# Projections chunk by chunk, a gating stage in another order, and an attention with ScalarE and VectorE in program order

## The chip, the cores and the metric

The kernel runs on one core of a Trainium2 chip. The metric is the device time in microseconds, as the median of several runs. TensorE (PE in the profile) does the matmuls and reads its weights with separate loads (PEld), VectorE (DVE) and ScalarE (ACT) do the elementwise work and read the matmuls' results, GpSimd (POOL) takes a part of the elementwise work in on-chip memory, and SyncE (SP) issues all transfers to and from HBM.

## What is computed

A trunk of two layers over 1024 latent tokens and 256 context tokens, 1024 wide, in float32. Both layers have the form x = layer_norm(alpha x + gate y).

```python
# layer 0: recurrent unit and spatial gating unit
p = h @ w_in                                   # 5 parts of 512
y_a = h_rec * silu(p[..., W:2 * W])            # bidirectional linear scan h_rec
u, v = gelu(p[..., 2 * W:3 * W]), gelu(p[..., 3 * W:4 * W])
y_b = spatial_gating(u, v) * silu(p[..., 4 * W:5 * W])
y = concatenate([y_a, y_b]) @ w_out
# layer 1: gated convolution and differential attention, 4 heads
p = h @ w_in                                   # 8 parts of 512
s = einsum('bqhmd,bkhmd->bhmqk', q, k) * d ** -0.5     # m = 0, 1
a = softmax(s[:, :, 0]) - lam * softmax(s[:, :, 1])
o = einsum('bhqk,bkhe->bqhe', a, v)            # k, v: context and latent tokens
y = concatenate([conv branch, rms_norm(o) * silu(gate)]) @ w_out
```

## The kernel before, in words

Every float32 operand of a matmul is split into two parts, a rounded one (hi, made by ScalarE) and the rest (lo, made by VectorE or GpSimd as a difference: `split`, L134). A product is then three matmuls: hi by hi, hi by lo, lo by hi. The input of a layer lies on chip with its features on the partitions: 8 blocks of 128 features (k), 1280 tokens in three chunks of 256, 512 and 512 (`CHUNKS`, L28).

A projection of 128 output features takes 8 x 3 x 3 = 72 matmuls. `proj3_g` (L158) runs over k outside, over the three products, and over the three chunks inside; it is used in layer 0. `proj1_g` (L170) does one chunk and runs over k; the keys and everything in layer 1 use it. `wload` (L143) loads the weights of a projection (512 KB, two raw buffers) and splits them in two halves of four k-blocks each, with four buffers of hi and four of lo; ScalarE makes hi, GpSimd lo.

TensorE issues in the order of the program text (`manual_schedule` at L55). The order on the other engines comes from a scheduler that simulates the program; nested regions at L305 and L514 fix SP's order as well. In such a region an engine issues its instructions in the order of the text.

Layer 0. `lru_x`, `lru_g` and `lru_rec` do the recurrent unit for four groups of features; `interleave` (L483) puts the steps of the modulation (`mod_step`) into the projections' gaps. Then the gating: z of group 0 (L520), the value weights (`vweights`), ten tiles of 128 tokens of v (`sgu_v`, L540, TensorE 24 matmuls a tile), the spatial products (`sgu_s`, L555) between them, the u projection of group 1 (L583) with the last spatial products inside, and then z of group 1, u and z of groups 2 and 3 (L620 to L627). Their results lie in two PSUM buffers of three banks (`pj3`).

Layer 1. Keys and values are projected and written to HBM. The attention (L1013) runs over 34 steps; step i of the first 32 is one block of 128 queries of a head, 8 blocks a head, in pairs that share their loaded queries (`load_q`, L902: two maps, hi and lo). `scores(i, m)` (L935) is six matmuls into one PSUM tile of three banks (psc, a single buffer), the row maximum on VectorE (L944) and the exponential on ScalarE (L946), which frees the tile. After m = 1 the two exponentials are combined on VectorE (L948 to L950, L1043). `trans(i - 1, .., j)` (L954) transposes the combined block before in three parts (4, 4 and 2 transposes; atr) and splits them (ah by ScalarE, al by VectorE). `av` (L968) multiplies a finished pair by the values; `finish1` to `finish3` normalise and gate half a head. `fill(us)` (L916) puts steps of the other projections (`proj_qg`, `conv_branch`) between, by the amounts in `FL` (L912); a step is three matmuls and counts 0.65 us. So a block has 0.1, 1.2, 1.0 and 0.5 us of fill around its three transpose steps, and either 1.3 with `av` or 4.7 between its two scores: 5.8 in the mean. Each weight is loaded where its projection begins. `load_k` and `load_v` load into one buffer (kd) and split at once.

## Time and profile before

| | us |
|---|---|
| median of 3 runs | 1170.89 (1170.02 to 1172.15) |
| span of the profiled execution | 1170.5 |
| layer 0, recurrent unit, until the z projection of group 0 | 0 to 209 |
| gating | 209 to 383 |
| output projection of layer 0, keys and values of layer 1 | 383 to 613 |
| attention with the other projections | 613 to 1071 |
| output projection of layer 1 | 1071 to 1170 |

The profile follows one execution. Its span of 1170.5 us is 0.4 under the median of the runs. Matmuls are pipelined: the profile gives each one from its start to its modelled end, so neighbours overlap, and the distance from start to start is the pace. PEclk is the clock that TensorE was granted, as a share of 2.4 GHz (0.5 is 1.2 GHz). A wait is given in brackets behind the instruction that waited, with what released it.

### The profile page before, as it was taken

What the parts mean: (1) busy time and instruction counts of PE and PEld (TensorE: products, weight loads), DVE (VectorE), ACT (ScalarE), POOL (GpSimd) and SP (SyncE); (2) the same over time, 40 slices, a digit from 0 to 9 for tenths busy, and PEclk for the clock granted to TensorE, in tenths of its full rate; (3) what the DMA queues carried; (4) which work ended last, traced back from release to release, by engine and by line L of the source; (5) the groups of instructions that cost most, each with busy time, mean ns of one, the idle gap of its engine ahead of it and who ended that gap; (6) DMA issues with size and microseconds to landing.
All of it is one profiled execution on the core that took longest, in us unless ns stands there. A gap on an engine that the chain in (4) does not pass through costs nothing.

```text
span 1170.5 us, 14967 instructions
## 1 busy us (share of the span) xinstructions
PE 1132.6 (97%) x5842; PEld 922.0 (79%) x5842; DVE 738.9 (63%) x1007; ACT 440.2 (38%) x685; POOL 329.6 (28%) x200
## 2 busy tenths in 40 slices
PE   6999999899999999999999899999999999999997
PEld 3667777678888888888887788788888788888776
DVE  5677986943411475636104668876777877738897
ACT  3453654621121234342113455544544554413110
POOL 1114212620240132258104311221121321221971
PEclk9999999999999999999999999999999999999999
DMA  9654551230332444243215411322221510126622
GB/s 373 239 182 142 180 176 41 73 130 1 120 104 71 144 139 147 96 136 140 77 45 162 113 55 54 95 76 84 77 76 37 146 62 19 46 72 249 218 99 82
DMA packets 71606, 133.93 MB, mean 114 GB/s; under 512 B 6368, under 2 KB 34912, under 8 KB 70640
## 3 DMA queue, kind: packets, MB, share of 16 engines
q1 hardware_dynamic: 71536, 132.97, 34.3%
q8 instruction: 46, 0.75, 0.3%
q14 instruction: 24, 0.20, 0.1%
HBM read 105.67 MB, written 27.28 MB: 114 GB/s over the span
## 4 chain that ended last, share of the span: by engine, by line
PE 83%; DVE 8%; DMA 3%; ACT 3%; issue 2%; POOL 0%; SPq 0%; POOLq 0%; DVEq 0%; ACTq 0%
PE px L164 5%; PE pu L164 5%; PE pg L164 5%; PE p L174 5%; PE p L175 5%; PE p L176 5%; PE pout L648 4%; PE pout L646 4%; PE pout L647 4%; PE pz L164 4%; PE psc L942 3%; PE pv L198 3%; PE pv L199 3%; PE pv L200 3%; PE psc L943 3%; PE atr L965 3%
## 5 line engine op out<-in xcount | busy, mean ns | idle before, releaser
L141 POOL TENSOR_TENSOR wlo<-wraw,whi 128x512 fp32r<-128x512 f32 x92 | 148.1, 1615 | 458.5 <-ACT whi L138 449.8
L648 PE MATMUL pout<-woh,ylo 128*128 128x512 f32 (+1 forms) x296 | 114.5, 387 | 3.1 <-DVE ylo L141 3.1
L946 ACT ACTIVATE e<-psc,st 128x1280 f32<-128x1280 f32 x64 | 85.1, 1329 | 85.6 <-DVE st L944 85.6
L646 PE MATMUL pout<-woh,yhi 128*128 128x512 f32 (+1 forms) x296 | 114.8, 388 | 0.2
L647 PE MATMUL pout<-wol,yhi 128*128 128x512 f32 (+1 forms) x296 | 114.0, 385 | 0.0
L944 DVE TENSOR_REDUCE st<-psc 128x1 f32<-128x1280 f32 x64 | 95.0, 1485 | 27.8 <-PE psc L943 27.7
L138 ACT ACTIVATE whi<-wraw 128x512 fp32r<-128x512 f32 x92 | 57.2, 628 | 134.3 <-PE p L175 27.7
L174 PE MATMUL p<-hhl,whi 128*128 128x512 f32 x256 | 106.8, 417 | 0.0
L176 PE MATMUL p<-hhl,wlo 128*128 128x512 f32 x256 | 100.7, 393 | 0.0
L175 PE MATMUL p<-hll,whi 128*128 128x512 f32 x256 | 100.5, 393 | 0.0
L942 PE MATMUL psc<-k,qh 128*128 128x512 f32 (+1 forms) x192 | 68.0, 369 | 8.4 <-ACT e L946 8.4
L943 PE MATMUL psc<-k,ql 128*128 128x512 f32 (+1 forms) x192 | 69.3, 361 | 0.0
L138 ACT ACTIVATE ah<-atr 128x512 fp32r<-128x512 f32 (+1 forms) x96 | 48.5, 525 | 51.6 <-PE atr L965 50.6
L648 PEld LDWEIGHTS pout<-woh,ylo 128*128 128x128 f32 x296 | 55.6, 188 | 15.3 <-DVE ylo L141 4.0
L646 PEld LDWEIGHTS pout<-woh,yhi 128*128 128x128 f32 x296 | 55.6, 188 | 12.1 <-DVE zt L610 0.5
L647 PEld LDWEIGHTS pout<-wol,yhi 128*128 128x128 f32 x296 | 55.7, 188 | 11.5
L138 ACT ACTIVATE yhi<-yraw 128x512 fp32r<-128x512 f32 x36 | 22.5, 630 | 103.7 <-PE pout L647 57.6
L141 DVE TENSOR_TENSOR al<-atr,ah 128x512 fp32r<-128x512 f32 (+1 forms) x96 | 55.6, 594 | 5.8 <-ACT ah L138 5.6
L176 PEld LDWEIGHTS p<-hhl,wlo 128*128 128x128 f32 x256 | 48.2, 188 | 10.7
L175 PEld LDWEIGHTS p<-hll,whi 128*128 128x128 f32 x256 | 48.6, 190 | 7.3
L141 DVE TENSOR_TENSOR ylo<-yraw,yhi 128x512 fp32r<-128x512 f32 x36 | 43.2, 1208 | 17.5 <-ACT yhi L138 17.5
L174 PEld LDWEIGHTS p<-hhl,whi 128*128 128x128 f32 x256 | 48.4, 189 | 7.2
(292 smaller groups left out, 2822.2 us busy)
## 6 DMA issues: line engine op xcount, KB each, us to landing
wraw<-in_w_in_dram SPq DMA_DIRECT2D x44, 512.0 KB, 3.7
wm<-in_w_mod_dram SPq DMA_DIRECT2D x64, 256.0 KB, 3.4
wraw<-in_w_out_dram SPq DMA_DIRECT2D x16, 512.0 KB, 3.5
wm<-in_w_mod_dram SPq DMA_DIRECT2D x7, 1024.0 KB
xt<-in_xcT_dram SPq DMA_DIRECT2D x8, 640.0 KB, 9.8
xres<-in_xc_dram SPq DMA_DIRECT2D x10, 512.0 KB, 3.7
kd<-k_d SPq DMA_DIRECT2D x16, 320.0 KB, 4.7
wvr<-in_w_v_dram SPq DMA_DIRECT2D x8, 512.0 KB, 4.4
```

Of the source, the lines that this page charges most:

```text
L138: S.activation(hi, src, AF.Copy)
L141: le.tensor_tensor(lo, src, f32(hi), op=ALU.subtract)
L164: T.matmul(o, wt[:, k % 4], hh[hx][:, k], start=st, stop=sp_)
L174: T.matmul(o, hi[:, k % 4], hh[:, k], start=k == 0, stop=False)
L175: T.matmul(o, hi[:, k % 4], hl_[:, k], start=False, stop=False)
L176: T.matmul(o, lo[:, k % 4], hh[:, k], start=False, stop=k == KT - 1)
L646: T.matmul(o, hi[:, i], wh[:, c], start=first and i == 0, stop=False)
L647: T.matmul(o, hi[:, i], wl[:, c], start=False, stop=False)
L648: T.matmul(o, lo[:, i], wh[:, c], start=False, stop=not first and i == 3)
L942: T.matmul(o, qh[:, m, cu], KS[m][:, c:c + n], start=True, stop=False)
L943: T.matmul(o, ql[:, m, cu], KS[m][:, c:c + n], start=False, stop=True)
L944: V.tensor_reduce(st[:, m:m + 1], p[:, 256:1536], axis=AX.X, op=ALU.max, negate=True)
```

## The change

The projections of layer 0 (but the first two) use a new `proj3c_g`, which finishes one chunk before it begins the next; the places at which other steps are put inside are moved to match. The u projection of group 1 runs right after z of group 0, ahead of the value tiles, with its weights loaded ahead of the value weights; the z projection of group 1 takes its old place. In the last groups the weights of a projection are loaded ahead of the output weights.

In the attention, steps 0 to 33 stand in a region in which ScalarE and VectorE issue in the order of the text (TensorE does so everywhere). The combination of the exponentials moves behind the three transposes of the step, and the load of a new pair's queries moves to the end of the odd step, behind the combination; it takes two transfers and not four. The first two transposes stand together, with their fill behind them. Keys and values are fetched one to two steps ahead of their split into two buffers, and the weights of the other projections one projection ahead (`ahead`).

```diff
...
+    def proj3c_g(ps, w):
+        for c0, n in CHUNKS:
+            o, (hh, hl_) = ps[:, 256 + c0:256 + c0 + n], hs(c0, n)
+            for k in range(KT):
+                hi, lo = w[k // 4]
+                T.matmul(o, hi[:, k % 4], hh[:, k], start=k == 0, stop=False)
+                T.matmul(o, hi[:, k % 4], hl_[:, k], start=False, stop=False)
+                T.matmul(o, lo[:, k % 4], hh[:, k], start=False, stop=k == KT - 1)
+                yield 0.68 * n / 512
     def proj3(ps, w):
-        run(proj3_g(ps, w))
+        run(proj3c_g(ps, w))
...
                 p = pj3("px")
-                PROJ(proj3_g(p, WX1 if f == 1 else wload(A["w_in0"][f])))
+                PROJ(proj3c_g(p, WX1 if f == 1 else wload(A["w_in0"][f])))
             else:
...
                 p = pj3("pg")
-                PROJ(proj3_g(p, wload(A["w_in0"][4 + f])))
+                PROJ(proj3c_g(p, wload(A["w_in0"][4 + f])))
             else:
...
             for i, _ in enumerate(gen):
-                if i in (1, 5):
+                if i in (9, 17):
                     mod_step()
...
         p = pj3("pu")
-        run(proj3_g(p, wload(A["w_in0"][8])))
+        proj3(p, wload(A["w_in0"][8]))
         S.activation(ut0, p[:, 256:1536], AF.Gelu_apprx_tanh)
...
     WZ0 = wload(A["w_in0"][12])
+    WU1 = wload(A["w_in0"][9])
     wv = vweights(vp, A["w_v0"], G, 3)
...
         VF = [vw.tile([128, 512], F32, name=f"vf{i}") for i in range(6)]
-        WU1 = wload(A["w_in0"][9])
         so_cm.__exit__(None, None, None)
         VH = {}
+        p = pj3("pu")
+        proj3(p, WU1)
+        ut1 = gp.tile([128, NTOK], F32, name="ut1", tag="ut", bufs=2)
+        S.activation(ut1, p[:, 256:1536], AF.Gelu_apprx_tanh)
...
         sgu_v(3)
+        WZ1 = wload(A["w_in0"][13])
         sgu_v(4, sgu_s((0, 1, 2)))
...
         sgu_v(9, sgu_s((6, 7)))
-        p = pj3("pu")
+        p = pj3("pz")
         s89 = sgu_s((8, 9))
-        for i, _ in enumerate(proj3_g(p, WU1)):
-            if 2 <= i < 6:
+        for i, _ in enumerate(proj3c_g(p, WZ1)):
+            if i in (8, 11, 14, 17):
                 next(s89)
-        ut1 = gp.tile([128, NTOK], F32, name="ut1", tag="ut", bufs=2)
-        S.activation(ut1, p[:, 256:1536], AF.Gelu_apprx_tanh)
+        zt1 = gp.tile([128, NTOK], F32, name="zt1", tag="ut", bufs=2)
+        S.activation(zt1, p[:, 256:1536], AF.Tanh, scale=0.5)
+        V.scalar_tensor_tensor(zt1, zt1, 1.0, p[:, 256:1536], op0=ALU.add, op1=ALU.mult)
         V.tensor_tensor(SS[0], SS[0], ut0, op=ALU.mult)
...
         SY.dma_start(yb_d[0], zt0)
+        V.tensor_tensor(SS[1], SS[1], ut1, op=ALU.mult)
+        V.scalar_tensor_tensor(zt1, zt1, 0.5, SS[1], op0=ALU.mult, op1=ALU.mult)
+        SY.dma_start(yb_d[1], zt1)
     vp_cm.__exit__(None, None, None)
     u0_cm.__exit__(None, None, None)
-
-    V.tensor_tensor(SS[1], SS[1], ut1, op=ALU.mult)
...
     YA = {}
-    for g in range(1, 4):
-        if g > 1:
-            sgu_u(g, wload(A["w_in0"][8 + g]))
+    for g in (2, 3):
+        w = wload(A["w_in0"][8 + g])
+        wo0.update(out_weights(woa, A["w_out0"], (2 * g - 4,)))
+        sgu_u(g, w)
         if g == 3:
...
                 YA[t] = y_load(y0, ya_d, 128 * t, 2)
-        wo0.update(out_weights(woa, A["w_out0"], (g - 1,)))
-        sgu_z(g, wload(A["w_in0"][12 + g]))
-    wo0.update(out_weights(woa, A["w_out0"], (3,)))
+        w = wload(A["w_in0"][12 + g])
+        wo0.update(out_weights(woa, A["w_out0"], (2 * g - 3,)))
+        sgu_z(g, w)
     gp_cm.__exit__(None, None, None)
...
+    order = [16, 24, 17, 25, 0, 8, 4, 12, 18, 26, 1, 9, 5, 13, 19, 27, 2, 10, 6, 14, 3, 11, 7, 15]
+    FW = []
+    def ahead():
+        if order:
+            FW.append(wload(A["w_in1"][order.pop(0)]))
+    ahead()
     def proj_qg(hd):
-        w = wload(A["w_in1"][16 + hd])
+        w = FW.pop(0)
         qf = rt("qf")
...
             yield from proj1_g(p, w, CTX + c0, 512)
+            if c0 == 0:
+                ahead()
             x = qf[:, c0:c0 + 512]
...
             SY.dma_start(q_d[hd][:, c0:c0 + 512], x)
-        w = wload(A["w_in1"][24 + hd])
+        w = FW.pop(0)
         sg = cs.tile([128, LAT], F32, name="sg8", tag="sg8", bufs=1)
...
             yield from proj1_g(p, w, CTX + c0, 512)
+            if c0 == 0:
+                ahead()
             s = sg[:, c0:c0 + 512]
...
         V.memset(tp[:, 1025:1026], 0.0)
-        w = wload(A["w_in1"][f])
+        w = FW.pop(0)
         for c0 in (0, 512):
...
             yield from proj1_g(p, w, CTX + c0, 512)
+            if c0 == 0:
+                ahead()
             S.activation(tp[:, 1 + c0:513 + c0], p, AF.Copy)
-        w = wload(A["w_in1"][8 + f])
+        w = FW.pop(0)
         for c0 in (0, 512):
...
             yield from proj1_g(p, w, CTX + c0, 512)
+            if c0 == 0:
+                ahead()
             V.tensor_tensor(tp[:, 1 + c0:513 + c0], p, tp[:, 1 + c0:513 + c0], op=ALU.mult)
...
                                    op1=ALU.add)
-        w = wload(A["w_in1"][4 + f])
+        w = FW.pop(0)
         for c0 in (0, 512):
...
             yield from proj1_g(p, w, CTX + c0, 512)
+            if c0 == 0:
+                ahead()
             V.scalar_tensor_tensor(u[:, c0:c0 + 512], p, 0.5, u[:, c0:c0 + 512], op0=ALU.mult, op1=ALU.mult)
-        w = wload(A["w_in1"][12 + f])
+        w = FW.pop(0)
         for c0 in (0, 512):
...
             yield from proj1_g(p, w, CTX + c0, 512)
+            if c0 == 0:
+                ahead()
             s = pp.tile([128, 512], F32, name="s3", tag="sh", bufs=2)
...
-    def load_k(hd, m):
-        kd = ap.tile([128, NTOK], F32, name="kd", tag="kd", bufs=1)
+    def fetch_k(hd, m):
+        kd = ap.tile([128, NTOK], F32, name="kd", tag="kd", bufs=2)
         for i in range(2):
             SY.dma_start(kd[64 * i:64 * i + 64], k_d[hd][64 * m:64 * m + 64])
+        KD[m] = kd
+    def load_k(m):
+        kd = KD.pop(m)
         kt = ap.tile([128, NTOK], F32R, name=f"k{m}")
...
-    def load_v(hd):
-        vf = ap.tile([128, NT, 128], F32, name="vf", tag="kd", bufs=1)
+    def fetch_v(hd):
+        vf = ap.tile([128, NT, 128], F32, name="vf", tag="kd", bufs=2)
         SY.dma_start(vf, v_d[:, :, 128 * hd:128 * hd + 128])
+        KD["v"] = vf
+    def load_v():
+        vf = KD.pop("v")
         vh = ap.tile([128, NT, 128], F32R, name="vh")
...
         for m in range(2):
-            for i in range(2):
-                SY.dma_start(qd[64 * i:64 * i + 64, m], q_d[hd][64 * m:64 * m + 64, 256 * pr:256 * pr + 256])
+            SY.dma_start(qd[64 * m:64 * m + 64], q_d[hd][:, 256 * pr:256 * pr + 256].rearrange("(m d) t -> d m t", m=2))
         qh = ap.tile([128, 2, 256], F32R, name="qh", tag="qh", bufs=2)
...
-    KS, VS, QS, AH, OF, SD = {}, {}, {}, {}, {}, {}
+    KS, VS, QS, AH, OF, SD, KD = {}, {}, {}, {}, {}, {}, {}
...
         S.activation(e_, p[:, 256:1536], AF.Exp, bias=st[:, m:m + 1], scale=1.0, accum_out=st[:, 2 + m:3 + m])
-        if m == 1:
-            V.reciprocal(st[:, 5:6], st[:, 3:4])
-            V.scalar_tensor_tensor(st[:, 6:7], st[:, 5:6], st[:, 2:3], nlam, op0=ALU.mult, op1=ALU.mult)
-            V.scalar_tensor_tensor(SD[i // 4][:, i % 4:i % 4 + 1], st[:, 2:3], EPS, st[:, 2:3], op0=ALU.mult,
-                                   op1=ALU.mult)
         return e_
+    def combine(i, st, e0, e1):
+        V.reciprocal(st[:, 5:6], st[:, 3:4])
+        V.scalar_tensor_tensor(st[:, 6:7], st[:, 5:6], st[:, 2:3], nlam, op0=ALU.mult, op1=ALU.mult)
+        V.scalar_tensor_tensor(SD[i // 4][:, i % 4:i % 4 + 1], st[:, 2:3], EPS, st[:, 2:3], op0=ALU.mult, op1=ALU.mult)
+        V.scalar_tensor_tensor(e0, e1, st[:, 6:7], e0, op0=ALU.mult, op1=ALU.add)
...
     fillers += [proj_qg(1), conv_branch(0), proj_qg(2), conv_branch(1), proj_qg(3), conv_branch(2), conv_branch(3)]
-    load_k(0, 0)
-    load_k(0, 1)
-    load_v(0)
+    fetch_k(0, 0)
+    load_k(0)
+    fetch_k(0, 1)
+    QS[0, 0] = load_q(0, 0)
+    load_k(1)
+    fetch_v(0)
     E0, fin = {}, None
+    at_cm = tc.manual_schedule(engines={nc.scalar.engine, nc.vector.engine})
+    at_cm.__enter__()
     for i in range(34):
...
         if i < 32:
-            if u == 0:
-                QS[hd, pr] = load_q(hd, pr)
             st = ap.tile([128, 8], F32, name="st", tag="st", bufs=3)
...
             if i % 8 == 7 and hd < 3:
-                load_k(hd + 1, 0)
+                load_k(0)
+        if i == 1:
+            load_v()
         if i > 1 and u == 1:
...
             if i % 8 == 1 and hd < 4:
-                load_v(hd)
+                load_v()
             fill(FL[2])
...
             fill(FL[3])
+        e1 = None
         if i < 32:
             e1 = scores(i, 1, st)
-            V.scalar_tensor_tensor(E0[i], e1, st[:, 6:7], E0[i], op0=ALU.mult, op1=ALU.add)
-            if i % 8 == 7 and hd < 3:
-                load_k(hd + 1, 1)
         fill(FL[4])
-        for j in range(3):
-            if 1 <= i < 33:
-                trans(i - 1, E0[i - 1], j)
-            fill(FL[5 + j])
+        for js, us in (((0, 1), FL[5] + FL[6]), ((2,), FL[7])):
+            for j in js:
+                if 1 <= i < 33:
+                    trans(i - 1, E0[i - 1], j)
+            fill(us)
+        if e1 is not None:
+            combine(i, st, E0[i], e1)
+        if i % 2 and i < 31:
+            QS[(i + 1) // 8, (i + 1) % 8 // 2] = load_q((i + 1) // 8, (i + 1) % 8 // 2)
+        if hd < 3:
+            if i % 8 == 5:
+                fetch_k(hd + 1, 0)
+            if i % 8 == 6:
+                fetch_k(hd + 1, 1)
+            if i % 8 == 7:
+                load_k(1)
+                fetch_v(hd + 1)
+    at_cm.__exit__(None, None, None)
     fill(FL[0])
...
```

## Rows read from the trace of the kernel before

**Rows 1.** The page's engine rows: busy time, share of span and instructions.

```profile
PE 1132.6 (97%) x5842; PEld 922.0 (79%) x5842; DVE 738.9 (63%) x1007; ACT 440.2 (38%) x685; POOL 329.6 (28%) x200
```

**Rows 2.** Waits, TensorE's: total us, number, longest.

```profile
PE psc L942 <- ACT e L946: 8.4, 6, 4.8
```

**Rows 3.** Timeline, TensorE, gating: start, us, line, names, shapes, count, wait.

```profile
223.30 0.39 PE L198 MATMUL pv<-wvh,hhc 128*128 128x512 f32 x1
...
236.71 0.61 PE L198 MATMUL pv<-wvh,hhc 128*128 128x512 f32 x1 [0.95 <-DVE zt L523]
...
240.46 0.39 PE L198 MATMUL pv<-wvh,hhc 128*128 128x512 f32 x1
```

**Rows 4.** Timeline, TensorE: ends of a gate projection and a key projection.

```profile
340.41 0.28 PE L164 MATMUL pz<-hhc,whi 128*128 128x256 f32 x1
...
354.41 0.28 PE L164 MATMUL pu<-hhc,whi 128*128 128x256 f32 x1
...
530.00 0.28 PE L174 MATMUL pk<-hhc,whi 128*128 128x256 f32 x1
...
543.74 0.28 PE L174 MATMUL pk<-hhc,whi 128*128 128x256 f32 x1
```

**Rows 5.** Timeline, start of attention, VectorE and then TensorE.

```profile
640.91 2.95 DVE L141 TENSOR_TENSOR ql<-qd,qh 128x512 fp32r<-128x512 f32 x1 [5.26 <-ACT qh L138]
...
646.76 0.58 PE L942 MATMUL psc<-k,qh 128*128 128x256 f32 x1 [4.77 <-ACT e L946]
```

**Rows 6.** Timeline, TensorE: second scores of blocks 1 and 31.

```profile
658.42 0.28 PE L942 MATMUL psc<-k,qh 128*128 128x256 f32 x1
...
1018.59 0.28 PE L942 MATMUL psc<-k,qh 128*128 128x256 f32 x1
```

**Rows 7.** Timeline, TensorE: a wait inside the attention.

```profile
758.41 0.38 PE L942 MATMUL psc<-k,qh 128*128 128x256 f32 x1 [1.94 <-ACT e L946]
```

**Rows 8.** Windows: length, busy PE, PEld, DVE, ACT, POOL; PEclk, DMA, GB/s.

```profile
646.00:650.00 4.00, 3.24 (x9) 2.66 (x10) 1.60 (x6) 1.20 (x3) 1.28 (x1) 0.57 0.77 196
759.00:767.00 8.00, 8.00 (x27) 6.62 (x26) 5.25 (x8) 2.66 (x5) 2.28 (x2) 0.57 0.30 96
```

**Rows 9.** Timeline, TensorE, blocks 5 and 6: four marks.

```profile
699.22 0.39 PE L174 MATMUL p<-hhl,whi 128*128 128x512 f32 x1
...
704.14 0.28 PE L942 MATMUL psc<-k,qh 128*128 128x256 f32 x1
...
705.30 0.60 PE L965 MATMUL atr<-ident,e 128*128 128x128 f32 x4
...
709.16 0.28 PE L942 MATMUL psc<-k,qh 128*128 128x256 f32 x1
```

**Rows 10.** Timeline of the same blocks, VectorE, then ScalarE.

```profile
705.50 1.49 DVE L944 TENSOR_REDUCE st<-psc 128x1 f32<-128x1280 f32 x1 [0.75 <-PE psc L943]
706.91 0.68 DVE L141 TENSOR_TENSOR ql<-qd,qh 128x512 fp32r<-128x512 f32 x1
...
708.11 0.68 DVE L141 TENSOR_TENSOR al<-atr,ah 128x512 fp32r<-128x512 f32 x1
708.70 0.15 DVE L948 RECIPROCAL st<-st 128x1 f32<-128x1 f32 x1
...
709.63 1.54 DVE L1043 SCALAR_TENSOR_TENSOR e<-e,st 128x1280 f32<-128x1280 f32 x1
711.09 0.42 DVE L141 TENSOR_TENSOR al<-atr,ah 128x256 fp32r<-128x256 f32 x1
...
705.99 0.60 ACT L138 ACTIVATE ah<-atr 128x512 fp32r<-128x512 f32 x1
707.02 1.33 ACT L946 ACTIVATE e<-psc,st 128x1280 f32<-128x1280 f32 x1 [0.43 <-DVE st L944]
```

**Rows 11.** Groups by form, VectorE, 658.42 to 1018.59: first and last filler group.

```profile
L853 DVE SCALAR_TENSOR_TENSOR uc<-tp,par,uc 128x1024 f32<-128x1024 f32 x6 | 7.7, 1284 | 0.1
...
L851 DVE TENSOR_SCALAR uc<-tp,par 128x1024 f32<-128x1024 f32 x3 | 2.2, 743 | 0.0
```

## What the change should do to the time

> **What bounds the kernel now.** I read first the page's engine rows, then TensorE's waits, then the timeline of each stretch that the change touches. TensorE is busy for 97% of the span [rows 1], so nothing that only relieves another engine pays; time can be won in three ways: waits in front of a matmul, stretches at the lower clock, and the pace from matmul to matmul. The list of waits has little left: 8.4 us in six waits of the score matmuls for the exponential [rows 2]. Two places show more than that list. In the first gating tile (t = 0) TensorE starts at 223.30 and reaches the next tile only at 236.71, and nine matmuls then take 3.75 us [rows 3]. At the start of attention it stands 4.77 us for the exponential, because VectorE does a 2.95 us split of queries (ql) ahead of the row maximum that is due [rows 5]. So in the attention what matters is the order on VectorE and ScalarE, and how long each lets TensorE stand.
>
> **Projections chunk by chunk.** Fourteen projections keep their matmuls and get another order. The one at 340.41 takes 14.00 us, and a key projection of the same 72 matmul shapes, already run chunk by chunk, takes 13.74 [rows 4]. The difference is 0.26 us. Seven of the fourteen run undisturbed: 1.8 us. The six of the RG-LRU and the gate projection of group 1 are cut by other matmuls; I give them half, 0.9. Bounds: nothing for these seven, or all of it: 1.8 to 3.6. I take **-2.7**. The weights of all eight k-blocks are now wanted within the first chunk and not over 14 us; in the kernel before they are split one projection ahead, so this costs nothing as long as that lead holds. The row says that order moves the pace. The Trainium skill (TensorE: Matmul & The Clock Gate, Back-to-back issue gap) has the gap between two matmuls depend on columns and clock alone; by it this term is nothing and the sum 2.7 us higher. The two rows differ, so I follow them.
>
> **Gating reordered.** TensorE meets the u projection of group 1 right after the z projection of group 0, where it used to meet tile 0. Tile 0 has 24 matmuls of 512 columns; at the key projection's pace (13.74 us for what is worth 60 such) that is 5.5 us, against 13.41 used: 7.9 lost. Nine matmuls behind it lose 3.75 - 2.06 = 1.7 [rows 3, 4]. The moved projection needs neither the value weights nor the buffer that VectorE frees late, and its 14 us reach from 223.3 to 237.3, past the 236.71 at which that buffer came free. So all of it goes: **-9.6**. Were the cover 3 us short (the weights of the projection pass ScalarE and GpSimd ahead of the value weights), a third would come back. The gate projection of group 1 takes over the place between tile 9 and the last spatial products, where the u projection stood, so nothing is uncovered. The SP queue carries one more 512 KB load ahead of the value weights; TensorE now wants those 14 us later.
>
> **Attention start.** With the maximum in program order, nothing can be put ahead of it: the 4.77 us go, and with them the clock drop behind it (1.2 GHz granted instead of 2.4; 0.57 in the mean over 4 us, which costs 0.43 x 4 = 1.7) [rows 5, 8]: **-6.5**. Were another wait to form there, up to all of it stays.
>
> **Attention, the steady part.** From the end of one odd block to the next, TensorE needs, over 15 pairs, 360.17 us [rows 6]. Of that 8.4 - 4.8 = 3.6 are waits [rows 2], and 0.43 x 8 = 3.4 the lower clock after the wait at 758.41 [rows 7, 8]. These **7.0** are what program order could win.
>
> What it costs is read from one block. Call T the end of the second scores of an odd block (705.30). TensorE comes to the next scores at 709.16, so at T + 3.86 [rows 9]; those scores start a new pair of blocks and want new queries. In the kernel before, VectorE splits these right behind the maximum (706.91), ahead of the combination of the two exponentials (709.63) [rows 10]. The change has VectorE in the order of the text: maximum, three splits of the transposed block before (al), combination, and only then the query split. ScalarE, also in order, does the exponential before the copies (ah) that these splits wait for, where it used to do one copy ahead of it. With the durations of [rows 10] from T: maximum 0.20 to 1.69; exponential 1.72 to 3.05; copy to 3.65; two splits of 512, which follow each other at 0.6 (0.68 each, overlapped), 3.74 to 4.95; split of 256 to 5.3; three small operations of 0.15 to 0.22 with their handoffs to 5.95; combination 5.95 to 7.5; query split 7.45 to 8.13; handoff 8.2. To this comes what the other projections leave on VectorE in that stretch: ten groups from 7.7 to 2.2 us, together 41.8 in 30 blocks [rows 11], 1.4 each, of which this stretch has 2.8/5.8 by the fill amounts: 0.7. The first matmul of the scores needs only the copy, so TensorE stands 8.9 - 3.86 - 0.12 = **4.9 us** at each of the 15 loads of queries, and the rest of TensorE's queue, projections among it, stands behind it. With no filler work in the stretch it is 4.2; with twice as much 5.6.
>
> The even block loads no queries. There the combination ends at 7.5 + 0.7, the next maximum runs to 9.65 and its exponential to 11.0; TensorE comes to the scores that want its bank at 3.86 + 1.16 + 4.92 = 9.94 [rows 9]: **1.1 us**, 0.4 without filler work. Together 6.0 x 15 = **+90**; bounds 4.6 x 15 = 69 and, with twice the filler work, 7.4 x 15 = 111.
>
> Waits of 4.77 and 1.94 us were each followed by the clock at half rate, 1.7 and 3.4 us of work lost [rows 5, 7, 8]. I take the smaller for each of the 15 long waits: **+25.8**; bounds 0 and 51. The same page of the Trainium skill (HAM oscillation — how this bites in real kernels) says that a wait which returns in every turn of a loop makes every turn start at the lower clock; by it the term is due 15 times. No row shows such a repetition.
>
> **At nothing.** Keys and values come early into two buffers, weights one projection ahead, queries by two transfers and not four: DMA waits of ScalarE, and only what reaches TensorE counts. SP keeps the scheduler's order and issues 32 fewer transfers. What is queued behind a late transfer is now all of ScalarE; the fetches stand one or two blocks (11 to 24 us) ahead of their use. A rope's last sum on VectorE waits for GpSimd with the maximum behind it: six times perhaps 2 us, kept for the upper end. Two transposes without a fill between them change nothing on TensorE.
>
> **The sum**, against the profiled execution of 1170.5 (0.4 below the median of the runs): 1170.5 - 2.7 - 9.6 - 6.5 - 7.0 + 90 + 25.8 = 1260.5, so 1261 as a median.
>
> **Rivals.** (a) The waits come but the clock holds: for it, two drops are little to go by; against it, the one wait as long as these was followed by one. 1235 with filler work, 1214 without. (b) Faster: the program order takes away the misplacements and the query split is in time. Then all four gains stay: 1144.7. It decides at whether the split's end comes before T + 4; against it, maximum, exponential, one copy and one split alone end at 4.4. For it only an order on VectorE other than the text's. (c) The gains and small new waits cancel, with waits of about 1.7 us per pair: 1170. (d) The chunk order or the moved projection doesn't do what it says: +12 on any of these.
>
> **How the numbers follow.** Forecast 0.54; (a) 0.28; (b) 0.15; (c) 0.03. Slower is the forecast and (a): 0.82; same 0.03; faster 0.15, where 0.2% is about what a measurement of this kernel can tell from no change. The range takes (a) with the least filler work and the moved projection gained in full, with some room, and at the top more filler work, ropes and longer drops, not all of them at their worst: 1205 to 1300. It leaves out (b) and (c).
>
> **What would show it.** Right: matmuls of psc with waits of 4 to 5 us, 15 times, released by VectorE's ql, each behind the combination; the granted clock at half rate after many of them; pairs of about 31 us; no wait between 223 and 238; projections of 13.7 to 13.8. Wrong: ql done before TensorE comes, or pairs under 25 us. If ql is late but the pairs are near 29.5, the clock term was wrong.

## The result: slower by 11%, and by half as much again as forecast

The changed kernel takes 1303.95 us in the median of four runs (1298.16 to 1307.77) against 1171.52 for the kernel before: a ratio of 1.1125, interval 1.1104 to 1.1145. The forecast was 1261, with a range that ends at 1300. Slower was right, and the wait that the prediction described is there; the size lies above its range. The profiled execution has a span of 1306.0 us.

Engine rows of the page and TensorE's waits (total us, number, longest) in the changed kernel; they answer to [rows 1] and [rows 2]:

```profile
PE 1182.9 (91%) x5842; PEld 956.9 (73%) x5842; DVE 735.3 (56%) x1007; ACT 431.3 (33%) x685; POOL 311.0 (24%) x200
...
PE psc L989 <- DVE ql L141: 44.4, 16, 5.6
...
PE psc L988 <- ACT qh L138: 32.8, 16, 5.3
```

The same 5842 matmuls keep TensorE busy for 50 us longer, and two waits are new: the second matmul of a score tile waits for ql from VectorE, as forecast, and ahead of it the first waits for qh from ScalarE, which the prediction did not have. The wait for the exponential has grown from 8.4 us in six waits to 20.4 in fifteen.

The steady part of the attention (from the second scores of block 1 to those of block 31, [rows 6]) carries nearly all of the loss. Windows over it: length, busy time of PE, PEld, DVE, ACT, POOL, then PEclk, DMA share, GB/s. First the kernel before, then the changed one:

```profile
658.42:1018.59 360.17, 355.44 (x1999) 302.51 (x1998) 272.67 (x380) 180.84 (x302) 73.18 (x49) 0.99 0.23 71
```

```profile
653.43:1152.30 498.87, 407.83 (x1998) 336.72 (x1998) 276.52 (x382) 174.83 (x306) 72.25 (x50) 0.88 0.16 52
```

Length less PE is the time in which TensorE stands: 4.7 us before, 91.0 after. The PE column itself grew from 355.4 to 407.8 us for the same matmuls, and PEclk fell from 0.99 to 0.88: most of that part is the clock (47 us, worked out below). So these waits cost twice, once as standing and once as slow matmuls behind them.

The timeline of one load of queries (end of block 3, start of block 4; start, us, engine, line), answering to [rows 9, 10]:

```profile
689.22 1.49 DVE L990 TENSOR_REDUCE st<-psc 128x1 f32<-128x1280 f32 x1 [2.98 <-PE psc L989]
...
692.66 0.38 PE L1012 MATMUL atr<-ident,e 128*128 128x128 f32 x2
...
693.08 1.16 ACT L138 ACTIVATE whi<-wraw 128x512 fp32r<-128x512 f32 x2
...
694.12 0.61 ACT L876 ACTIVATE tp<-p 128x512 f32<-128x512 f32 x1
694.59 0.40 ACT L138 ACTIVATE ah<-atr 128x256 fp32r<-128x256 f32 x1
694.86 0.66 ACT L138 ACTIVATE qh<-qd 128x512 fp32r<-128x512 f32 x1
695.03 0.42 DVE L141 TENSOR_TENSOR al<-atr,ah 128x256 fp32r<-128x256 f32 x1 [0.99 <-ACT ah L138]
...
695.57 0.38 PE L988 MATMUL psc<-k,qh 128*128 128x256 f32 x1 [2.52 <-ACT qh L138]
...
696.34 1.55 DVE L999 SCALAR_TENSOR_TENSOR e<-e,st 128x1280 f32<-128x1280 f32 x1
697.81 0.68 DVE L141 TENSOR_TENSOR ql<-qd,qh 128x512 fp32r<-128x512 f32 x1
...
698.55 0.58 PE L989 MATMUL psc<-k,ql 128*128 128x256 f32 x1 [2.60 <-DVE ql L141]
...
698.93 0.63 PE L988 MATMUL psc<-k,qh 128*128 128x512 f32 x1
```

VectorE goes as the prediction said: maximum, splits, combination (696.34), and only then ql (697.81). ScalarE has its own queue ahead of qh: the weights of another projection (whi), a result of one (tp), the last copy of the transposed block (ah). TensorE stands 2.52 us for qh and 2.60 for ql, 5.1 together. The last line lasts 0.63 us where a matmul of that shape at full clock has 0.39 to 0.40.

Three of the stretches at half rate, as windows of the changed kernel:

```profile
696.20:703.00 6.80, 4.45 (x11) 3.58 (x12) 3.79 (x5) 0.60 (x1) 0.09 (x1) 0.51 0.38 116
...
924.90:938.60 13.70, 9.04 (x25) 7.33 (x26) 6.44 (x11) 4.75 (x10) 3.12 (x3) 0.50 0.13 37
...
993.20:1006.90 13.70, 8.38 (x24) 7.03 (x25) 5.73 (x10) 1.42 (x2) 2.70 (x3) 0.50 0.30 97
```

All three are at the lower of the two levels, 1.2 GHz, and each begins in the wait of a load. In the steady part 16 such stretches begin: one at each of the 15 loads and one at a wait of 3.2 us for the exponential (to 820.47). They are 3.4 to 13.7 us long, together 113 us, part of it spent standing. The other waits for the exponential have none.

### The profile page after: what moved, and what is told of

Read it like the earlier page. It is cut to its first block, busy times and chain, and to the rows that moved or that the text cites. A ratio compares the mean times of both kernels' runs of the same rounds, so it can differ in the third digit from the quotient of the medians.

```text
span 1306.0 us, 14857 instructions
## 1 busy us (share of the span) xinstructions
PE 1182.9 (91%) x5842; PEld 956.9 (73%) x5842; DVE 735.3 (56%) x1007; ACT 431.3 (33%) x685; POOL 311.0 (24%) x200
## 5 line engine op out<-in xcount | busy, mean ns | idle before, releaser
L141 POOL TENSOR_TENSOR wlo<-wraw,whi 128x512 fp32r<-128x512 f32 x92 | 130.1, 1427 | 587.1 <-ACT whi L138 574.0
L988 PE MATMUL psc<-k,qh 128*128 128x512 f32 (+1 forms) x192 | 78.3, 419 | 53.3 <-ACT qh L138 32.8
L989 PE MATMUL psc<-k,ql 128*128 128x512 f32 (+1 forms) x192 | 80.7, 420 | 44.4 <-DVE ql L141 44.4
L184 PE MATMUL p<-hhl,whi 128*128 128x512 f32 x256 | 111.4, 435 | 0.0
L185 PE MATMUL p<-hll,whi 128*128 128x512 f32 x256 | 106.2, 415 | 0.0
L186 PE MATMUL p<-hhl,wlo 128*128 128x512 f32 x256 | 105.6, 412 | 0.0
L988 PEld LDWEIGHTS psc<-k,qh 128*128 128x128 f32 x192 | 40.8, 213 | 71.4 <-ACT qh L138 38.9
L989 PEld LDWEIGHTS psc<-k,ql 128*128 128x128 f32 x192 | 42.4, 221 | 52.5 <-DVE ql L141 47.6
L664 PEld LDWEIGHTS pout<-woh,yhi 128*128 128x128 f32 x296 | 56.0, 189 | 12.4 <-DVE zt L627 0.5
L184 PEld LDWEIGHTS p<-hhl,whi 128*128 128x128 f32 x256 | 52.7, 206 | 9.8
L185 PEld LDWEIGHTS p<-hll,whi 128*128 128x128 f32 x256 | 52.4, 205 | 9.8
L138 ACT ACTIVATE yhi<-yraw 128x512 fp32r<-128x512 f32 x36 | 22.5, 630 | 112.0 <-PE pout L665 71.7
## 6 DMA issues: line engine op xcount, KB each, us to landing
xt<-in_xcT_dram SPq DMA_DIRECT2D x8, 640.0 KB, 10.2
```

The costliest lines, as they stand in the source:

```text
L138: S.activation(hi, src, AF.Copy)
L141: le.tensor_tensor(lo, src, f32(hi), op=ALU.subtract)
L184: T.matmul(o, hi[:, k % 4], hh[:, k], start=k == 0, stop=False)
L185: T.matmul(o, hi[:, k % 4], hl_[:, k], start=False, stop=False)
L186: T.matmul(o, lo[:, k % 4], hh[:, k], start=False, stop=k == KT - 1)
L664: T.matmul(o, hi[:, i], wh[:, c], start=first and i == 0, stop=False)
```

## The experiments

Two theories. **W**: the time goes where TensorE stands for the new pair's queries, which both engines' program order puts behind other work, and in the lower clock that follows. **R**: program order on ScalarE and VectorE costs as such; behind any wait that is removed stands the next.

**e1: the queries earlier.**

```diff
+        if i % 2 and i < 31:
+            QS[(i + 1) // 8, ...] = load_q(...)
         e1 = scores(i, 1, st)
 ...
         combine(i, st, E0[i], e1)
-        if i % 2 and i < 31:
-            QS[(i + 1) // 8, ...] = load_q(...)
```

> One move in the changed kernel: the queries of the next pair are loaded and split ahead of the second scores of the odd block, not behind its combination. ScalarE and VectorE stay in program order. Theory W (the time goes where TensorE stands for the new queries, 32.8 us for qh and 44.4 us for ql, and in the lower clock behind those waits): nearly all of the 77 us go, and of the some 60 us that the lower clock costs about 45; at the places that are freed, a wait for the exponential as in the even blocks may form, up to 15 x 1.1 = 16 us. 1304 - 77 - 45 + 16 = 1198, between 1170 and 1215. Rival R (program order on the two engines costs as a whole; behind the query stands the next late operation): the waits move to the maximum or the exponential, the clock still drops, and the time stays above 1245.

1233.49 us, ratio 1.0527 (1.0504 to 1.0550). TensorE's wait in e1:

```profile
PE psc L988 <- ACT e L992: 47.0, 30, 4.1
```

The time lies between the two forecasts, in neither. The waits for queries are gone but for one of 3.1 us at the start of the attention, and 70 us with them, so W names the larger part. But 30 waits for the exponential are there now, where W gave 16 us. R is right about this half: with the queries early, every block, and not only every second, shows the maximum that stands behind the combination.

**e2: the layer-0 edits alone**, with the attention of before.

> The kernel before with the layer-0 edits alone: the projections chunk by chunk and the gating reordered; the attention as before. In the trace of the changed kernel these stages ended 8.7 us earlier than before. Theory W: 1171.5 - 8.7 = 1163. The prediction on record had 12.3 us for them, 1159. Rival (what is won ahead of the attention is lost again at its start, as in the changed kernel, where the first scores stood 3.3 us and the third 4.3 us): 1167 to 1171.

1160.00 us, ratio 0.9903 (0.9875 to 0.9931): 1% faster. Nothing is given back at the start of the attention. Its steady part has TensorE at full clock all the way and serves as the measure below:

```profile
649.64:1006.03 356.39, 352.25 (x2000) 299.99 (x1999) 272.37 (x380) 180.83 (x302) 72.96 (x49) 1.00 0.24 72
```

**e3: the scheduler's order back** on ScalarE and VectorE, all else as changed.

```diff
-    at_cm = tc.manual_schedule(engines={nc.scalar.engine, nc.vector.engine})
-    at_cm.__enter__()
 ...
-    at_cm.__exit__(None, None, None)
```

> The changed kernel without the program order on ScalarE and VectorE in the attention: all else (early fetches of keys, values and weights, the place of the query loads and of the combination in the text) stays. Theory W: the scheduler puts the query splits ahead of the combination again, the waits of 77 us and the clock drops go: 1155 to 1175. Rival (the new places in the text or the early loads cost of themselves): above 1200.

1161.37 us, ratio 0.9914 (0.9891 to 0.9936). So 142.6 us hang on this one region; without it the early fetches and the new places in the text cost little: e3 is 1.4 us above e2, and the runs of the two overlap.

**e4: the stand filled with work.**

```diff
         p = pa.tile([128, 1536], F32, name="psc", tag="psc", bufs=1)
+        if m == 0 and i % 2 == 0 and i:
+            for r in range(50):
+                T.matmul(p[:, 0:256], hhl[:, 0, 0:128], hhl[:, 1, 0:256], ...)
```

> The changed kernel with 50 matmuls of 256 columns more ahead of the first scores of each of 15 pairs, written to a part of the bank that nothing reads; about 50 x 0.109 = 5.5 us each, about as long as TensorE stands there. They need nothing that is late, so the stand becomes work. If the stands bring the lower clock about, it stays at 2.4 GHz there and the time falls although work is added: 1304 + 15 x 0.4 - 50 = 1260, between 1245 and 1275. If the lower clock has another cause, the time is 1304 to 1312 and the drops are still there.

1291.56 us, ratio 1.1030 (1.0994 to 1.1067): 12.4 us under the changed kernel, with 750 matmuls more. Timeline of one load and window of the steady part in e4:

```profile
691.04 6.23 PE L988 MATMUL psc<-hhl 128*128 128x256 f32 x50
...
697.10 0.28 PE L991 MATMUL psc<-k,qh 128*128 128x256 f32 x1
```

```profile
652.51:1135.46 482.95, 457.06 (x2749) 400.23 (x2749) 276.62 (x382) 174.98 (x306) 72.71 (x50) 0.98 0.18 54
```

The clock stays up (0.98 against 0.88), so the standing does bring the lower clock about. The account on the steady part, at this load's pace: 50 matmuls take 697.10 - 691.04 = 6.06 us, so 15 x 6.06 = 90.9 of work more; standing 91.0 down to 482.95 - 457.06 = 25.9; and the other matmuls, 407.8 in the changed kernel, take 457.06 - 90.9 = 366.2, 41.6 less. 90.9 - 65.1 - 41.6 = -15.8, and 498.87 - 482.95 is 15.9. The time fell by less than expected on all three: 90.9 us of work and not 82.5, 65 us of standing gone and not 77, 42 us of matmul time back and not 50.

**e5: e1, and the combination behind the next block's first maximum.**

```diff
             E0[i] = scores(i, 0, st)
+            if late:
+                combine(*late)
 ...
-        if e1 is not None:
-            combine(i, st, E0[i], e1)
```

> The changed kernel with two moves: the next pair's queries ahead of the second scores, as in e1, and each block's combination behind the first row maximum of the next block and not ahead of it. ScalarE and VectorE stay in program order. In e1, 30 waits for the exponential were left, 47 us together, with 16 us of matmuls at half rate. Theory: those come from the combination that stands ahead of the maximum on VectorE; with it behind, they go, and a pair takes 23.6 to 24 us as in the kernel before: 1233 - 15 x 4.4 = 1167, between 1157 and 1175. Rival (the program order on the two engines costs as such, and the next late operation takes its place): above 1195.

1200.63 us, ratio 1.0243 (1.0224 to 1.0261): 33 us better than e1, but on the rival's side of the line. Half of the 30 waits are gone, so the combination made these; 22.5 us in 15 are left. Timeline around one of the longest in e5:

```profile
754.16 2.96 POOL L141 TENSOR_TENSOR vl<-vf,vh 128x1280 fp32r<-128x1280 f32 x1 [4.92 <-ACT vh L138]
754.64 3.03 DVE L141 TENSOR_TENSOR ql<-qd,qh 128x512 fp32r<-128x512 f32 x1 [0.93 <-ACT qh L138]
757.59 1.48 DVE L990 TENSOR_REDUCE st<-psc 128x1 f32<-128x1280 f32 x1
...
760.63 0.38 PE L988 MATMUL psc<-k,qh 128*128 128x256 f32 x1 [2.61 <-ACT e L992]
```

VectorE's query split, 0.68 us otherwise, takes 3.03 while GpSimd splits the values, and the maximum stands behind it. e11 tests this.

**e6: the query load one step earlier**, ahead of the combination.

```diff
+        if i % 2 and i < 31:
+            QS[(i + 1) // 8, ...] = load_q(...)
         if e1 is not None:
             combine(i, st, E0[i], e1)
-        if i % 2 and i < 31:
-            QS[(i + 1) // 8, ...] = load_q(...)
```

> The changed kernel with the query load one step earlier, ahead of the combination and still behind the transposed block's splits. VectorE then splits the queries as soon as ScalarE has made qh. Theory (two waits in a row, one for each engine's queue): the wait for ql, 2.8 us a pair, shrinks to some 0.6; the wait for qh, 2.2 us, stays; the combination ends 0.7 later, which the next wait for the exponential feels. 15 x (-2.2 + 0.5) = -25, and with shorter stands less of the lower clock, 5 to 20 us of the 43: 1304 - 25 - 12 = 1267, between 1255 and 1280. Rival (the prediction's reading: only VectorE's queue decides): the whole wait of 5 us goes, with the clock, 1215 or less.

1262.18 us, ratio 1.0766 (1.0739 to 1.0793), 42 us less than the changed kernel. Waits in e6:

```profile
PE psc L988 <- ACT qh L138: 33.1, 16, 5.3
...
PE psc L989 <- DVE ql L141: 16.2, 16, 3.7
```

As expected of two waits in a row: ql falls from 44.4 to 16.2, qh stays at 33.

**e9 and e10: program order on one engine alone.**

```diff
-    at_cm = tc.manual_schedule(engines={nc.scalar.engine, nc.vector.engine})
+    at_cm = tc.manual_schedule(engines={nc.vector.engine})      # e9
+    at_cm = tc.manual_schedule(engines={nc.scalar.engine})      # e10
```

> The changed kernel with program order on VectorE alone; ScalarE gets the scheduler's order. The prediction read its whole wait from VectorE's order (the query split behind the combination); the trace of the changed kernel showed a second cause under it, qh late on ScalarE. If VectorE's order decides: qh comes early, but ql still behind the combination, so the wait of some 5 us per pair stays, now all of it for ql: 1270 to 1300. If ScalarE's order is what counts: below 1230.

> The changed kernel with program order on ScalarE alone; VectorE gets the scheduler's order. qh then stays 2.2 us late per pair (33 us), and VectorE splits the queries as soon as qh is there, 0.6 more. Waits of 2.8 x 15 = 42 for the queries and less than 20 for the exponential, and 10 to 20 us of half rate: 1161 + 42 + 10 + 15 = 1228, between 1205 and 1250. If ScalarE's order does nothing by itself: 1160 to 1175.

e9: 1264.25 us, ratio 1.0765 (1.0726 to 1.0803). e10: 1255.75 us, ratio 1.0697 (1.0671 to 1.0723). One load in e9, then one in e10:

```profile
683.62 0.36 PE L988 MATMUL psc<-k,qh 128*128 128x256 f32 x1
687.31 0.58 PE L989 MATMUL psc<-k,ql 128*128 128x256 f32 x1 [3.33 <-DVE ql L141]
```

```profile
686.14 0.38 PE L988 MATMUL psc<-k,qh 128*128 128x256 f32 x1 [2.53 <-ACT qh L138]
...
687.80 0.58 PE L989 MATMUL psc<-k,ql 128*128 128x256 f32 x1 [1.27 <-DVE ql L141]
```

With VectorE alone in order qh is in time and the whole wait is ql's, 55.3 us in all; with ScalarE alone, qh's 27.4 and ql's 30.7. Each engine's order costs about 100 us by itself against e3 (102.9 and 94.4), both together 142.6, so they lie partly over each other. Both runs fell outside what was expected, e9 by 6 us below and e10 by 6 above: the reading "VectorE decides" holds in e9, but it is half of the matter.

**e7: chunk order alone.**

> The kernel before with the projections chunk by chunk and nothing else. Theory of the prediction: eight undisturbed projections 0.26 us shorter each, 2.1, and something of those that are cut by other matmuls, 2.7 in all, so the value projection of layer 1 begins about 2.5 us earlier than before. Rival: the cut projections give nothing, 1.8 to 2.1. Against the whole set of layer-0 edits (8.8 us) the rest is the gating's: 6 to 7 us where the prediction had 9.6.

1168.14 us, one run. From the first z matmul to the first query projection the three kernels need 404.2 us (before), 402.8 (e7) and 394.5 (e2). So chunk order gives 1.4 there and the gating 8.3; the kernels that share the layer 0 of e2 spread over 394.4 to 395.1.

**e8: the start of the attention**, e5 with the first queries loaded ahead of the second keys and the transfers there in the order of the text.

> e5 with one more edit: at the start of the attention the transfers are issued in the order of the text, and the first queries are loaded ahead of the second keys. In the changed kernel the queue issued the first queries behind two more key fetches and a weight load, and TensorE stood 3.3 us for qh. Theory: this wait goes, 3 us less than e5: 1155 to 1172. Rival: the second keys become late in its place, and the time is that of e5.

1196.30 us, ratio 1.0211 (1.0186 to 1.0236). The wait of 3.5 us for the first qh is gone, and the kernel is 4.3 us under e5, where 3 were expected (one of its four runs, 1201.35, lies among those of e5). The range had been set from the forecast for e5, which was too low.

**e11: e8 with the values split behind the transposes.**

```diff
-        if i == 1:
-            load_v()
 ...
-            if i % 8 == 1 and hd < 4:
-                load_v()
             fill(FL[2])
 ...
                     trans(i - 1, E0[i - 1], j)
             fill(us)
+        if i % 8 == 1 and hd < 4:
+            load_v()
```

> e8 with one move: the split of each head's values goes from in front of the second scores to behind the transposes of the same block. In e5 VectorE's query split took 3.03 us where it takes 0.68, from 754.64 and 968.61, and ended when GpSimd's split of the values (2.96 us from 754.16, 2.94 from 968.14) ended; the row maximum was behind it and TensorE stood 2.6 to 4.4 us at the same place of each head. Theory: VectorE's operations on SBUF stand still beside a GpSimd operation, and in program order the maximum stands with them; moved, the four waits shrink below 1 us: 4 x 2.5 and some 5 us of half rate less, 1196 - 15 = 1181, between 1172 and 1188. Rival: another operation behind the transposes is stretched in its place and the time is that of e8.

1186.35 us, ratio 1.0119 (1.0103 to 1.0136): 10 us less. The same place of the same head in e11, VectorE and GpSimd:

```profile
742.16 0.22 DVE L997 SCALAR_TENSOR_TENSOR st<-st,lv 128x1 f32<-128x1 f32 x1
...
744.48 0.68 DVE L141 TENSOR_TENSOR ql<-qd,qh 128x512 fp32r<-128x512 f32 x1
...
750.14 1.48 DVE L990 TENSOR_REDUCE st<-psc 128x1 f32<-128x1280 f32 x1
750.57 2.93 POOL L141 TENSOR_TENSOR vl<-vf,vh 128x1280 fp32r<-128x1280 f32 x1 [10.46 <-ACT vh L138]
...
751.72 1.79 DVE L997 SCALAR_TENSOR_TENSOR st<-st,lv 128x1 f32<-128x1 f32 x1
```

The query split is back at 0.68 us and the wait at this place is gone. The operation that meets GpSimd's split now is a small one (L997, 1.79 us where it takes 0.22), behind the maximum and not ahead of it.

**e12: e3 with the start of e8.**

> e3 (the scheduler's order on ScalarE and VectorE) with the start of e8: the transfers at the start of the attention in the order of the text, the first queries ahead of the second keys. In e3 TensorE stood 3.2 us for the first queries, and its steady part took 359.7 us against 356.4 with the attention before. Theory: the 3.2 us go: 1161.4 - 3 = 1158, as with the layer-0 edits alone (1160). Rival: the scheduler orders the steady part differently for it and loses as much, 1161 to 1166.

1163.11 us, ratio 0.9920 (0.9903 to 0.9937): no gain on e3. The first wait goes and another comes. Timeline of e12:

```profile
629.44 2.93 POOL L141 TENSOR_TENSOR vl<-vf,vh 128x1280 fp32r<-128x1280 f32 x1 [10.60 <-ACT vh L138]
630.43 2.48 DVE L141 TENSOR_TENSOR ql<-qd,qh 128x512 fp32r<-128x512 f32 x1 [2.41 <-ACT qh L138]
...
633.43 1.48 DVE L990 TENSOR_REDUCE st<-psc 128x1 f32<-128x1280 f32 x1
...
636.41 0.58 PE L988 MATMUL psc<-k,qh 128*128 128x256 f32 x1 [5.22 <-ACT e L992]
```

It is the stall of [rows 5] again: a query split put ahead of the maximum and stretched beside GpSimd.

## Why the size was wrong, step by step

The account of the profiled executions, in us, before (1170.5) to after (1306.0):

| part | forecast | measured |
|---|---|---|
| layer 0, from the first z matmul to the first query projection | -12.3 | -9.4 |
| start of the attention, to the second scores of block 1 | -6.5 | +3.7 |
| steady part: TensorE stands | +86.4 | +86.3 |
| steady part: the same matmuls take longer | +22.4 | +52.4 |
| ahead of the first z matmul, and behind block 31 | 0 | +2.5 |
| sum | +90.0 | +135.5 |

(86.4 is the forecast's 90 less the 3.6 of old waits; 22.4 its 25.8 less the 3.4 of old clock loss.)

**The waits** came out as worked out. The 15 loads wait 29.7 us for qh (32.8 less the 3.1 of the first load) and some 44 for ql, 4.9 each as forecast; the waits for the exponential, less one of 4.1 at the start, are 16.3 against 16.5. That the size came out is in part luck, since the picture of ScalarE was wrong. Its sentence that the first matmul "needs only the copy" took qh as there in time; e6, where ql comes early, still waits 30 us for qh (33.1 less 2.9 at the start). And filler work was counted on VectorE alone: in the load shown above, ScalarE does whi and tp ahead of the last ah, so the last split of the transposed block begins at 695.03, 6.0 us behind the scores where the sum has 4.95, and the combination and ql follow it.

**The clock** is the term that failed: 25.8 forecast, 1.7 for each load, and 47.3 measured, 3.2 for each. Windows over all stretches at half rate in the steady part (the 16 and the end of one that began ahead of it), their sum in the changed kernel:

```profile
sum 118.02, PE 94.61 PEld 77.60 DVE 49.52 ACT 23.36 POOL 15.89; mean PE 5.57 PEld 4.56 DVE 2.91 ACT 1.37 POOL 0.94
```

TensorE was busy for 94.6 us at half the clock; at full clock that work takes half, so 47.3 are lost. The prediction had two rows to go by, 1.7 and 3.4 us [rows 5, 7, 8], and took the smaller for no reason that it gave; the larger gives its upper bound, 51, close to what came. Against the 352.25 us that the matmuls of this part take at full clock (e2), the changed kernel needs 407.8 - 352.3 = 55.6 more. The 8.3 that are not the clock's are a cost that the prediction did not have: with 45 stands of over 0.1 us they come to 0.2 a stand, and e3, with no stretch at half rate, has the same 0.2 (1.2 us for six). Neighbouring matmuls overlap in the profile and those on either side of a wait do not, which is the likely reason; it was not tested.

So of the 45.5 us by which the sum fell short, the clock has 21.5 (47.3 less the 3.4 of before, against 22.4), the rest of the longer matmuls 8.5, the start of the attention 10.2, layer 0 2.9 and the ends 2.5. By the same reckoning the kernels with fewer waits need:

| kernel | TensorE stands | matmuls longer than in e2 | PEclk |
|---|---|---|---|
| changed | 91.0 | 55.6 | 0.88 |
| e9, VectorE alone in order | 69.6 | 39.0 | 0.91 |
| e6, queries before the combination | 64.1 | 39.1 | 0.93 |
| e10, ScalarE alone in order | 56.7 | 45.2 | 0.91 |
| e1, queries early | 48.6 | 24.3 | 0.95 |
| e5, and combination late | 27.7 | 14.3 | 0.97 |
| e11, and values late | 22.4 | 10.6 | 0.98 |
| e3, scheduler's order | 6.2 | 1.2 | 1.00 |

A microsecond of standing brought 0.5 to 0.8 more in longer matmuls wherever the waits returned, and 0.2 where they were few. The prediction weighed a section of the Trainium skill (TensorE: Matmul & The Clock Gate, HAM oscillation — how this bites in real kernels): a wait that returns in every turn of a loop makes every turn start slow. The trace agrees for the loads: each of the 15 has its stretch. The prediction took the count from this and the price from too small a row.

**The start of the attention** was forecast at -6.5. The 4.77 us of [rows 5] did go. Two others came, in the changed kernel:

```profile
621.18 1.10 SPq L927 DMA_DIRECT2D kd<-k_d  x2
622.33 0.58 SPq L145 DMA_DIRECT2D wraw<-in_w_in_dram  x1
623.01 1.90 SPq L952 DMA_DIRECT2D qd<-q_d  x3
...
629.71 0.38 PE L988 MATMUL psc<-k,qh 128*128 128x256 f32 x1 [3.10 <-ACT qh L138]
...
647.92 0.69 DVE L767 TENSOR_TENSOR qf<-qf,sh 128x512 f32<-128x512 f32 x1 [1.19 <-POOL qf L766]
...
650.45 1.48 DVE L990 TENSOR_REDUCE st<-psc 128x1 f32<-128x1280 f32 x1
...
653.43 0.58 PE L988 MATMUL psc<-k,qh 128*128 128x256 f32 x1 [4.11 <-ACT e L992]
```

The early fetches are the first: SP, still in the scheduler's order, issues key fetches and a weight load ahead of the first queries. The prediction had written "at nothing" for them and counted only the transfers that SP saves. e8 takes this wait away. The second is the rope: its last sum on VectorE waits for GpSimd, the combination and the maximum stand behind it. The prediction named it as "perhaps 2 us" for the upper end, and that is its size: with the combination moved behind the maximum (e5), the wait at this place is 2.22 us, so of the 4.11 the combination has the other 1.9. Behind both waits the clock fell to half rate, from 631.5 and from 652.0.

**Layer 0.** Undisturbed projections take what was forecast (13.74 us, from 318.48 to 332.22 in the changed kernel, against 14.00), so order moves the pace. The section of the Trainium skill that the prediction weighed (TensorE: Matmul & The Clock Gate, Back-to-back issue gap) has no term for order; the traces of both kernels show one, of 0.26 us in 14. Those cut by other matmuls gave nothing: 1.4 us in e7 from the first z matmul on, and ahead of it nothing that stands out, since the first z matmul of one and the same code came anywhere from 207.5 to 210.0. The gating gave 8.3 and not 9.6. VectorE and TensorE in the kernel before (first line) and in the changed one:

```profile
235.18 1.47 DVE L523 SCALAR_TENSOR_TENSOR zt<-zt,pz 128x1280 f32<-128x1280 f32 x1
...
233.97 3.67 DVE L438 TENSOR_TENSOR gt<-tt 128x256 f32<-128x256 f32 x2
237.57 1.48 DVE L534 SCALAR_TENSOR_TENSOR zt<-zt,pz 128x1280 f32<-128x1280 f32 x1
...
239.10 0.50 PE L208 MATMUL pv<-wvh,hhc 128*128 128x512 f32 x1 [1.51 <-DVE zt L534]
```

The first value tile still takes the buffer of z of group 0. VectorE freed it at 236.7 before [rows 3]; now VectorE does two products of the recurrent unit first, where it did one, and begins the one that frees it (zt) only at 237.57, so "all of it goes" was wrong by the 1.5 us of this wait. The step took a time of the kernel before as fixed, though the order on VectorE is the scheduler's and came out anew.

**The rivals.** (a), the waits without the clock, falls by PEclk 0.88 and by e4. (b), queries in time, is not what the changed kernel does, but it is what e3 does: 1161, not 1144.7, since of the 13.5 us forecast for the attention almost nothing was won there (start 45.2 us against 45.0 before, steady part 359.7 against 360.2). (c) falls; of the 12 us of (d), 2.9 came.

Open: why the half-rate stretches last 3.4 us after one load and 13.7 after another. No run varied that alone. Not run either: the program order around the attention's text of before, so what the region costs without the new places of the query load and the combination is not known.

## What to carry to other kernels

Program order on an engine makes every late operation late for all that stands behind it, so follow each operand of the next matmul through the queue of the engine that makes it, not only the last one to arrive. A wait of TensorE that returned in the loop cost one and a half to nearly twice its length here (table above); price it so, and not at its length. A load whose data are long there belongs ahead of the step that it would otherwise wait behind: moving one such line (e1) won half of what the region had cost. The best version here keeps only the layer-0 edits (e2, 1160.0) or adds the fetches without the region (e3, 1161.4), both below the kernel before.

## What the runs showed of the hardware

Filling each stand with 50 useless matmuls, some 91 us of work in place of 65 us of standing, still made the changed kernel faster (e4): the other matmuls got 41.6 us shorter, and PEclk rose from 0.88 to 0.98.

A VectorE operation with two operands in SBUF that begins behind a GpSimd operation which reads there stands still until that one ends: 3.03 us for 0.68 (e5, from 754.64), ending 0.55 us behind GpSimd's; 1.79 for 0.22 (e11). Begun first, it keeps its time and GpSimd's grows: in the kernel before, the combination from 652.79 took its usual 1.55 us, and a GpSimd split from 652.99 took 2.50 where it takes 1.29. The row maximum, which reads PSUM, kept its 1.48 us beside the same split (e11, from 750.14, GpSimd from 750.57). The Trainium skill (SBUF — State Buffer, Who interferes with whom) says that a VectorE instruction with two SBUF inputs contends with a GpSimd instruction that reads SBUF, that the order of issue decides which of them waits, and that one with at most one SBUF input does not contend outside its two-port modes; the rows agree.
